# One decoder layer on one core: transfers at other places, two first tiles split from PSUM, squares of x later, last squares in two parts

## The chip, the cores and the metric

The kernel runs on one core of a Trainium2 chip. A core has a matrix engine (PE, with a queue of its own for weight loads, PEld), a vector engine (DVE), an activation engine (ACT), a general engine (POOL) and a queue engine (SP). SP's and POOL's DMA instructions move data between DRAM and the core's SBUF, over 16 DMA engines that all queues share. PE writes its results to PSUM, which DVE and ACT read. The metric is the device time of one execution in microseconds (us), as the median over several runs.

## The reference

One step of a hybrid decoder layer on 512 prompt tokens and 8 single tokens of running sequences, all in float32. Cut to what matters:

```
x = concat(x_prompt (1, 512, 2048), x_sample (8, 1, 2048))
proj = rmsnorm(x, norm_mix_g) @ w_in                 # 2048 -> 6160 columns
bg, cg, hin, q, k, v, og, glr = split(proj)
cu, conv_new = causal_dwconv(cg * hin, conv_prev, conv_w)     # width 3
ya = bg * cu                                         # 1024 columns
o, s_new = gla_chunked(q, k, v, log_sigmoid(glr @ gate_w2 + gate_b) / 16, gla_prev)
yb = rmsnorm(o per head) * gla_norm_g * silu(og)     # 4 heads, 1024 columns
x = x + concat(ya, yb) @ w_out
u, v = split(rmsnorm(x, norm_ffn_g) @ w_up)          # 2 x 5632 columns
cu, ffn_new = causal_dwconv(u, ffn_prev, ffn_conv_w)
x = x + (silu(cu + b) * v) @ w_down                  # 5632 -> 2048
y = rmsnorm(x, final_norm_g)
```

It also returns the new states. Those of the sample tokens (`new_conv_s`, `new_ffn_s`, two rows each) hold in row 0 what was row 1 of the old state: a copy from DRAM to DRAM.

## The kernel before

Tokens are columns: x and all that follows lies transposed, features on the 128 partitions, 520 tokens along, in two halves of 260. Each float32 operand is split in two parts of lower precision, hi and lo, and a product takes three matmuls (hi by hi, lo by hi, hi by lo). ACT makes hi by a copy, DVE makes lo as the difference. So each weight tile of 128 x 1024 (512 KB) passes ACT and DVE once before PE uses it.

The order of the instructions on PE, DVE and ACT is the order of the program text, cut in steps by calls of `in_order()`. The queues of SP and POOL run down their own lists, each instruction as soon as its data and its buffer are there.

**Start.** x arrives on SP's queue: the first 512 features in four loads (`x0` to `x3`), the others in three loads of 1 MB (`xc`). For each tile k of 128 features `x_copy(k)` has PE transpose the four blocks and the sample rows into a PSUM tile `tp` (2 buffers) and copies it to SBUF as `t`: on ACT for k < 4 (L382), on DVE after that. `x_split(k)` stores the copy to DRAM on POOL's queue (`xT_d`, L388; the residual reads it later) and splits it, scaled by the norm's weight `gm`: hi on ACT (L126, `bh` and `ch` for the two halves), lo on DVE (L127, `bl` and `cl`). `parts` splits a weight tile (L111, L112). The loop over k then runs 12 matmuls for each tile (L140), copies a tile ahead, splits another, and takes squares of x for the norm; those of the first 512 features are taken on POOL at k = 0 to 3, in place in `x0` to `x3` (L472). `warm(n)` issues n matmuls whose results are not used.

**Heads and convolution tiles** follow, and then 81 groups of seven products each, by a scheme that needs seven products of blocks in place of eight: 9 groups for the rest of `w_in` (mix), 8 for `w_out` (wo), 44 for `w_up` (up), 20 for `w_down` (down: 5 chunks c of input features by 4 groups g of output columns, written (c, g)). A product is 24 matmuls of 260 columns. `begin(n + 1)` at the first product (j = 0) of group n allocates and loads the four raw weight tiles of the next group: `weights` issues the tile (1,1) (L1140), `second_half` the two tiles (2,1) and (2,2) (L754); the tile (1,2) follows at j = 2 (`load_rest`, L1182). `prepare(i + 2)` makes hi (L1199), lo (L1203) and sums of tiles (L1144) two products ahead. For the first mix group the second half is loaded early, in the step before (`early`), and the sums of inputs that it multiplies come from DRAM as `yl<-mt_d` (L1579).

Before the group stage the two state copies (176 KB and 32 KB, L1109) are issued on POOL's queue.

**Down.** A product's inputs come from DRAM as `form` (L648, SP's queue). Results are added into 16 accumulators `acc[g, q]` in SBUF. The residual is added into them by DMA, with accumulation in the DMA, four for each g (`add_residual`, L1439, POOL's queue, from `x1_d`), at places given by (c, g) and j:

```
if j == 5 and (c, g) in ((1, 0), (1, 1), (1, 2), (2, 2)):
    add_residual("down", {0: 2, 1: 3}.get(g, c - 1))
```

Behind the last residual POOL's queue has `load_last`, eight loads of the last four tiles (L1446). Those four tiles of 44 are not in the groups; they run at the end in the usual way.

**End.** `half` runs the last products for a part of the tokens, adds the accumulators, transposes each tile of 128 features back (L1806), and after every fourth tile squares 512 columns on ACT with a sum (L1814). After m = 15 the sums are reduced (L1848), and the rows are scaled and stored.

## Time and profile before

| | |
|---|---|
| time before, median of 3 runs | 2170.77 us (2170.47 to 2171.22) |
| the profiled execution | 2170.91 us, of which its span is 2169.2 us |
| PE busy | 2137.6 us (99%) |
| DVE busy | 1735.3 us (80%) |
| ACT busy | 1112.6 us (51%) |
| POOL busy | 440.2 us (20%) |
| bytes moved by DMA | 415.51 MB, mean 192 GB/s |
| DMAs of the residual in the down stage (L1439) | 16 of 260.0 KB, 6.8 us to landing |

All times in the views count from the start of the span. [...] `[1.71 <-ACT ms L1233]` behind a row means that the engine was idle for 1.71 us before it and that the named instruction ended the idle time. A row with `x24` stands for 24 instructions in a run. In the tables of loads, the last number is the median time from issue to landing.

### The profile page before, as it was taken

What the parts mean: (1) busy time and instruction counts of PE and PEld (TensorE: products, weight loads), DVE (VectorE), ACT (ScalarE), POOL (GpSimd) and SP (SyncE); (2) the same over time, 40 slices, a digit from 0 to 9 for tenths busy, and PEclk for the clock granted to TensorE, in tenths of its full rate; (3) what the DMA queues carried; (4) which work ended last, traced back from release to release, by engine and by line L of the source; (5) the groups of instructions that cost most, each with busy time, mean ns of one, the idle gap of its engine ahead of it and who ended that gap; (6) DMA issues with size and microseconds to landing.
All of it is one profiled execution on the core that took longest, in us unless ns stands there. A gap on an engine that the chain in (4) does not pass through costs nothing.

```text
span 2169.2 us, 43815 instructions
## 1 busy us (share of the span) xinstructions
PE 2137.6 (99%) x17751; PEld 2114.4 (97%) x17751; DVE 1735.3 (80%) x2298; ACT 1112.6 (51%) x1625; POOL 440.2 (20%) x625
## 2 busy tenths in 40 slices
PE   9999999999999999999999999999999999999997
PEld 8999999999999998999999999999999999999997
DVE  6446465578888898998898998998998877888886
ACT  6335435345554577555555555555555553444445
POOL 4213131212243421121221131122111310010000
PEclk9999999999999999999999999999999999999999
DMA  8545464387898997667676676676677886894734
GB/s 248 144 129 156 125 187 121 99 241 204 208 258 248 297 269 188 175 179 190 166 189 177 166 196 177 166 199 174 174 185 189 292 204 192 249 272 135 227 108 157
DMA packets 467163, 415.51 MB, mean 192 GB/s; under 512 B 21641, under 2 KB 426393, under 8 KB 466817
## 3 DMA queue, kind: packets, MB, share of 16 engines
q1 hardware_dynamic: 424081, 289.71, 46.8%
q0 software_dynamic: 42832, 122.93, 21.6%
q8 instruction: 139, 2.28, 0.4%
q14 instruction: 63, 0.52, 0.1%
q10 hardware_dynamic: 48, 0.07, 0.0%
HBM read 299.45 MB, written 80.31 MB: 175 GB/s over the span
## 4 chain that ended last, share of the span: by engine, by line
PE 60%; DMA 2%; DVE 1%; issue 1%; ACT 0%; POOL 0%; ACTq 0%; DVEq 0%; POOLq 0%; SPq 0%
PE mm L1223 28%; PE ms L1223 11%; PE y L1466 7%; PE x L1466 6%; PE e L1466 2%; PE f L1466 2%; PE mm L140 2%; DMA x_d<-acc 1%; DMA ssq<-fh 1%; DMA raw<-in_w_down_dram 0%; PE ms L1806 0%; DVE lo L1203 0%; DVE yl L124 0%; ACT y L1864 0%; DVE s L1144 0%
## 5 line engine op out<-in xcount | busy, mean ns | idle before, releaser
L1223 PE MATMUL mm<-yl,hi 128*128 128x260 f32 x1696 | 477.2, 281 | 4.1 <-DVE yl L124 4.1
L1223 PE MATMUL mm<-yh,hi 128*128 128x260 f32 x1696 | 476.5, 281 | 1.9 <-ACT ms L1233 1.7
L1223 PE MATMUL mm<-yh,lo 128*128 128x260 f32 x1696 | 475.8, 281 | 1.3 <-DVE lo L1203 1.3
L1199 ACT ACTIVATE hi<-raw 128x1024 fp32r<-128x1024 f32 x324 | 342.0, 1056 | 243.7 <-issue 88.3
L1203 DVE TENSOR_TENSOR lo<-raw,hi 128x1024 fp32r<-128x1024 f32 x324 | 395.5, 1221 | 43.6 <-ACT hi L1199 40.6
L1203 DVE TENSOR_TENSOR lo<-s,hi 128x1024 fp32r<-128x1024 f32 x243 | 298.4, 1228 | 124.1 <-ACT hi L1199 123.8
L1199 ACT ACTIVATE hi<-s 128x1024 fp32r<-128x1024 f32 x243 | 257.5, 1059 | 222.6 <-PE ms L1223 93.9
L1223 PEld LDWEIGHTS mm<-yl,hi 128*128 128x128 f32 x1696 | 320.3, 189 | 4.9 <-DVE yl L124 4.9
L1223 PEld LDWEIGHTS mm<-yh,hi 128*128 128x128 f32 x1696 | 320.0, 189 | 2.3 <-ACT ms L1233 1.9
L1223 PEld LDWEIGHTS mm<-yh,lo 128*128 128x128 f32 x1696 | 319.7, 188 | 1.7 <-DVE lo L1203 1.7
L1223 PE MATMUL ms<-b,hi 128*128 128x260 f32 x1408 | 265.7, 280 | 0.0
L1223 PEld LDWEIGHTS ms<-b,hi 128*128 128x128 f32 x1408 | 222.6, 188 | 0.0
L1466 PE MATMUL y<-form,hi 128*128 128x260 f32 x1120 | 212.7, 282 | 1.3 <-DVE acc L1485 1.3
L1466 PE MATMUL x<-form,hi 128*128 128x260 f32 x1120 | 211.5, 281 | 0.1
L1144 DVE TENSOR_TENSOR s<-s,raw 128x1024 f32<-128x1024 f32 x162 | 197.9, 1222 | 2.8
L1223 PE MATMUL ms<-b,lo 128*128 128x260 f32 x704 | 197.9, 281 | 0.0
L1466 PEld LDWEIGHTS y<-form,hi 128*128 128x128 f32 x1120 | 177.6, 189 | 1.8 <-ACT hi L1199 0.8
L1466 PEld LDWEIGHTS x<-form,hi 128*128 128x128 f32 x1120 | 176.6, 188 | 0.7 <-issue 0.5
L1466 PE MATMUL y<-form,lo 128*128 128x260 f32 x560 | 157.4, 281 | 2.2 <-DVE lo L1203 2.2
L1466 PE MATMUL x<-form,lo 128*128 128x260 f32 x560 | 156.7, 280 | 0.3 <-DVE lo L1203 0.3
L112 DVE TENSOR_TENSOR lo<-raw,hi 128x1024 fp32r<-128x1024 f32 x76 | 93.1, 1231 | 75.3 <-ACT hi L111 75.3
L1223 PEld LDWEIGHTS ms<-b,lo 128*128 128x128 f32 x704 | 132.0, 188 | 0.0
(366 smaller groups left out, 5074.1 us busy)
## 6 DMA issues: line engine op xcount, KB each, us to landing
raw<-in_w_up_dram SPq DMA_DIRECT2D x176, 512.0 KB, 4.9
raw<-in_w_down_dram SPq DMA_DIRECT2D x96, 512.0 KB, 5.6
raw<-in_w_in_dram SPq DMA_DIRECT2D x92, 512.0 KB, 4.7
form<-f_d SPq DMA_DIRECT2D x126, 260.0 KB, 6.2
raw<-raw POOLq DMA_DIRECT2D x56, 512.0 KB, 5.8
f_d<-t POOLq DMA_DIRECT2D x80, 260.0 KB, 5.6
raw<-in_w_out_dram SPq DMA_DIRECT2D x32, 512.0 KB, 9.1
form<-g_d POOLq DMA_DIRECT2D x42, 260.0 KB, 7.4
```

Of the source, the lines that this page charges most:

```text
L112: nc.vector.tensor_tensor(lo, raw, hi.bitcast(F32), op=ALU.subtract)
L140: nc.tensor.matmul(o, w, xx, start=first and i == 0, stop=last and i == 2)
L1144: return lambda: nc.vector.tensor_tensor(out, x, y, op=ALU.add)
L1199: nc.scalar.activation(his[i], src, AF.Copy)
L1203: nc.vector.tensor_tensor(los[i], src, his[i].bitcast(F32), op=ALU.subtract)
L1223: nc.tensor.matmul(st["bank"][b], w[:, k, :], x, start=b not in st["used"] and k == 0 and j == 0, stop=k == 7 and j == 2, skip_group_check ...
L1466: nc.tensor.matmul(ps[:, m, :], w[:, k, m * P : (m + 1) * P], x, start=b not in st["used"] and k == 0 and j == 0, stop=k == 3 and j == 2, ...
```

## The change

Six edits, in the order of the program:

1. For k = 0 and 1 the hi part is computed on DVE from the PSUM tile (a multiplication by `gm`), and lo on DVE from the copy; ACT makes only the copy. The matmuls of k = 0 stand ahead of the loop as `first_pass(w, x)` (w and x: 0 is hi, 1 is lo), two passes before the transposes of tile 1 and one behind them. `warm(8)` is `warm(7)`.
2. The squares of the first 512 features on POOL are taken at k = 8 to 11.
3. The two state copies are issued in the up stage, at the product with index NW + 70 (NW is the index of the first up product).
4. The first mix group's raw tile (1,1) is loaded ahead of the second half and of two other loads.
5. The residual of the down stage is added at other places: for g = 1 at j = 1 of (1, 2), for g = 0, 2, 3 at j = 1 of (2, 1).
6. The squares of the last 512 columns at the end are taken in two parts, 384 columns after m = 14 and 128 after m = 15.

```diff
-            st = copies[k] = tmp()[:, :T]
+            st = tmp()[:, :T]
+            copies[k] = st, ps
...
-            if k < KD // 2:
+            if k < 2:
+                his, los = xa[k]
+                for hi, x in zip(his, halves(ps)):
+                    nc.vector.tensor_scalar(hi, x, gm[:, k : k + 1], None, op0=ALU.mult)
+                for hi, lo, x in zip(his, los, halves(st)):
+                    nc.vector.scalar_tensor_tensor(
+                        lo, x, gm[:, k : k + 1], hi.bitcast(F32),
+                        op0=ALU.mult, op1=ALU.subtract,
+                    )
+            elif k < KD // 2:
...
+        def first_pass(w, x):
+            for i, ps in enumerate(first):
+                for o, xx in zip(ps, xa[0][x]):
+                    nc.tensor.matmul(
+                        o[:, :HT], ws[0][w][:, 4 * i, :], xx, start=w == x == 0, stop=False
+                    )
...
-        warm(8)
+        warm(7)
         ws = [parts(raws[0], 8)]
+        first_pass(0, 0)
+        first_pass(0, 1)
         x_copy(1)
         x_split(1)
+        first_pass(1, 0)
...
-            for i, ps in enumerate(first):
+            for i, ps in enumerate(first if k else ()):
...
-            if c == 0:
+            if 8 <= k < 12:
                 nc.gpsimd.tensor_tensor(xc[0][t], xc[0][t], xc[0][t], op=ALU.mult)
-            elif c < 3:
+            if 0 < c < 3:
                 square(c, t)
...
-    for dst, src in ((new_conv_s, state_conv), (new_ffn_s, state_ffn_conv)):
-        nc.gpsimd.dma_start(dst[0, :, 0, :], src[0, :, 1, :])
...
     raws = [load_og(2), load_og(3)]
-    early = second_half(lambda m, k: mix_source(0, m, k))
+    w11, first = raw_tile(lambda m, k: mix_source(0, m, k), 1)
+    nc.sync.dma_start(*first)
+    early = {(1, 1): w11, **second_half(lambda m, k: mix_source(0, m, k))}
...
+        if i == NW + 70:
+            for dst, src in ((new_conv_s, state_conv), (new_ffn_s, state_ffn_conv)):
+                nc.gpsimd.dma_start(dst[0, :, 0, :], src[0, :, 1, :])
...
-            if j == 5 and (c, g) in ((1, 0), (1, 1), (1, 2), (2, 2)):
-                add_residual("down", {0: 2, 1: 3}.get(g, c - 1))
+            if j == 1:
+                for q in {(1, 2): (1,), (2, 1): (0, 2, 3)}.get((c, g), ()):
+                    add_residual("down", q)
...
-            if m % 4 == 3:
+            if m % 4 == 3 or m == KD - 2:
                 b = m // 4
+                c0, c1 = (0, 512) if b < 3 else ((0, 384), (384, 512))[m % 2]
                 for i, (u0, un) in enumerate(tiles):
                     junk = tmp()
+                    n = b + (c0 > 0)
                     nc.scalar.activation(
-                        junk[:un, :512], pt[0][i][:un, :], AF.Square,
-                        accum_out=sums[:un, i, b : b + 1],
+                        junk[:un, c0:c1], pt[0][i][:un, c0:c1], AF.Square,
+                        accum_out=sums[:un, i, n : n + 1],
                     )
```

`raw_tile` only allocates a tile of `weights` and names its source. Line numbers shift: L382 becomes L383, L1140's load of the first mix group L1648, L754 L774, L1182 L1206, L1579 L1603, L1439 L1463.

How the order on the engines changes, at three places. The first is ACT at the start, before:

```order
L382 ACTIVATE t<-tp 128x520
L126 ACTIVATE bh<-t,gm 128x260
L126 ACTIVATE ch<-t,gm 128x260
L111 ACTIVATE hi<-raw 128x1024
L382 ACTIVATE t<-tp 128x520
L126 ACTIVATE bh<-t,gm 128x260
L126 ACTIVATE ch<-t,gm 128x260
```

The same place of ACT in the change:

```order
L383 ACTIVATE t<-tp 128x520
L111 ACTIVATE hi<-raw 128x1024
L383 ACTIVATE t<-tp 128x520 x2
L126 ACTIVATE bh<-t,gm 128x260
L126 ACTIVATE ch<-t,gm 128x260
```

The hi part of the first weight tile moved ahead of the splits, two of which went to DVE. On PE the row of work at the start reads in the change:

```order
L360 MATMUL mm<-ones 128x128 x7
L460 MATMUL mm<-bh,hi 128x260
L460 MATMUL mm<-ch,hi 128x260
L460 MATMUL mm<-bh,hi 128x260
L460 MATMUL mm<-ch,hi 128x260
L460 MATMUL mm<-bl,hi 128x260
L460 MATMUL mm<-cl,hi 128x260
L460 MATMUL mm<-bl,hi 128x260
L460 MATMUL mm<-cl,hi 128x260
L378 MATMUL tp<-idn,x_142 128x128 x4
L379 MATMUL tp<-idn,xs 128x8
L460 MATMUL mm<-bh,lo 128x260
```

Before, the transposes of tile 1 (L378, L379) stood ahead of all products of tile 0; now eight of these stand before them and four behind them.

The second place is SP's queue at the start of the mix groups, before:

```order
L101 DMA raw<-in_w_in_dram 128x8x128 x6
L754 DMA raw<-in_w_in_dram 128x8x128 x2
L1626 DMA t<-o_d 128x520 x2
L1140 DMA raw<-in_w_in_dram 128x8x128
L1182 DMA raw<-in_w_in_dram 128x8x128
L1579 DMA yl_5224<-mt_d 128x520
```

And in the change:

```order
L101 DMA raw<-in_w_in_dram 128x8x128 x6
L1648 DMA raw<-in_w_in_dram 128x8x128
L774 DMA raw<-in_w_in_dram 128x8x128 x2
L1652 DMA t<-o_d 128x520 x2
L1206 DMA raw<-in_w_in_dram 128x8x128
L1603 DMA yl_5221<-mt_d 128x520
```

The load of tile (1,1) moved past four other loads.

The third place is POOL's queue in the down stage. Here the rows have the numbers of the tiles: before, 20909 to 20912 are the accumulators of g = 0, 21157 to 21160 of g = 1, 21390 to 21393 of g = 2, 21615 to 21618 of g = 3. Six rows of the sixteen, before:

```order
L1439 DMA acc_21393<-x1_d_117 128x2x260
L1439 DMA acc_21615<-x1_d_117 128x2x260
L1439 DMA acc_21616<-x1_d_117 128x2x260
L1439 DMA acc_21617<-x1_d_117 128x2x260
L1439 DMA acc_21618<-x1_d_117 128x2x260
L1439 DMA acc_20909<-x1_d_117 128x2x260
```

In the change the numbers are 20908 to 20911 for g = 0, 21156 to 21159 for g = 1, 21389 to 21392 for g = 2, 21614 to 21617 for g = 3:

```order
L1463 DMA acc_21159<-x1_d_117 128x2x260
L1463 DMA acc_20908<-x1_d_117 128x2x260
L1463 DMA acc_20909<-x1_d_117 128x2x260
L1463 DMA acc_20910<-x1_d_117 128x2x260
L1463 DMA acc_20911<-x1_d_117 128x2x260
L1463 DMA acc_21389<-x1_d_117 128x2x260
```

The sixteen DMAs stand behind each other on POOL's queue in both kernels; their sequence by g was 2, 3, 0, 1 and is now 1, 0, 2, 3.

## The prediction

> **What bounds the kernel now.** I read the page's busy times first, then a table of windows over the stretches that the change touches, and only then single rows of the timeline, the chain of waits and the DMA issues there.

> ```profile
> span 2169.2 us, 43815 instructions
> PE 2137.6 (99%) x17751; PEld 2114.4 (97%) x17751; DVE 1735.3 (80%) x2298; ACT 1112.6 (51%) x1625; POOL 440.2 (20%) x625
> ```

> PE, the matrix engine, is busy for 2137.6 of 2169.2 us. So 31.6 us of idle PE is all that a reordering can win back, beside time in which PE is busy at a lower clock or ahead of its first useful product. The windows (length, busy time and instructions of PE, weight load, DVE, ACT and POOL, then granted clock, DMA share, GB/s) say how much of that lies where the change works.

> ```profile
> 12.00:27.00 15.00, 13.74 (x92) 11.31 (x91) 12.55 (x15) 8.23 (x18) 7.52 (x10) 1.00 1.10 358
> 27.00:58.00 31.00, 30.43 (x245) 28.68 (x245) 23.53 (x41) 21.93 (x45) 16.15 (x45) 1.00 0.64 191
> 446.00:455.00 9.00, 9.00 (x78) 9.00 (x77) 2.60 (x4) 0.64 (x1) 0.78 (x2) 1.00 1.09 270
> 458.00:476.00 18.00, 14.41 (x101) 13.60 (x101) 16.69 (x21) 11.68 (x19) 0.00 (x0) 0.91 0.92 284
> 470.00:475.00 5.00, 5.00 (x32) 5.00 (x31) 5.00 (x6) 2.70 (x5) 0.00 (x0) 0.66 0.72 177
> 1798.00:1805.00 7.00, 4.78 (x27) 4.58 (x26) 6.25 (x7) 2.11 (x2) 1.81 (x2) 0.76 1.10 358
> ```

> At the start of the mix groups (458 to 476) PE is idle for 18.00 - 14.41 = 3.59 us, and after it the clock is 0.66 for 5 us. In the down stage one stretch of 7 us has 7.00 - 4.78 = 2.22 us of idle PE and a clock of 0.76. In both the DMA share is near or above 0.9. In 12 to 27, PE looks 92% busy, but its 15 us hold little work, as the rows below show.

> **The start: k = 0 and 1 split from PSUM, first products ahead of the loop, squares later.** The columns are start, duration, engine, line and operation, out and in, and the idle time before it with its releaser.

> ```profile
> 6.37 0.60 ACT L382 ACTIVATE t<-tp 128x520 f32<-128x520 f32 x1 [3.12 <-PE tp L379]
> 6.63 0.71 SPq L319 DMA_DIRECT2D xc<-in_x_prompt_dram  x1
> 7.83 1.04 ACT L111 ACTIVATE hi<-raw 128x1024 fp32r<-128x1024 f32 x1
> 8.93 0.39 PE L140 MATMUL mm<-bh,hi 128*128 128x260 f32 x1
> 12.16 0.38 PE L140 MATMUL mm<-bh,hi 128*128 128x260 f32 x1
> 16.47 0.60 PE L378 MATMUL tp<-idn,xc 128*128 128x128 f32 x4
> 18.73 0.60 PE L378 MATMUL tp<-idn,xc 128*128 128x128 f32 x4
> 19.53 0.66 PE L378 MATMUL tp<-idn,xc 128*128 128x128 f32 x4
> 20.05 1.66 DVE L127 SCALAR_TENSOR_TENSOR bl<-t,gm,bh 128x260 fp32r<-128x260 f32 x1 [0.58 <-ACT bh L126]
> 20.37 1.05 POOL L472 TENSOR_TENSOR x<-x 128x512 f32<-128x512 f32 x1
> 25.90 0.47 DVE L127 SCALAR_TENSOR_TENSOR bl<-t,gm,bh 128x260 fp32r<-128x260 f32 x1
> 27.05 0.39 PE L140 MATMUL mm<-bh,hi 128*128 128x260 f32 x1
> 29.26 0.39 PE L140 MATMUL mm<-bh,hi 128*128 128x260 f32 x1
> ```

> Before, ACT ran the copy of tile 0 (ends 6.97), two hi splits, and the hi part of the first weights at 7.83; PE's first product waited for that (8.93). With the two hi splits on DVE, ACT starts the weights at about 7.0, 0.8 earlier, and the first product stands near 8.1. From there PE has work without a gap: eight products of k = 0 (about 0.12 each, 24 to a 2.87 us row below, so 0.95), the transposes of tile 1 (0.80, as 18.73 to 19.53), four products with the low weights (0.47) and the transposes of tile 2 (0.80): k = 1 begins at 8.1 + 0.95 + 0.80 + 0.47 + 0.80 = 11.1 in place of 12.16, or -1.05. DVE pays for it with four short instructions for each of two tiles; they stand where DVE waited for ACT's hi, and the fall-back, if they delay the low weights, is a gain of 0, which I keep as the upper end.

> From k = 1 (12.16) to k = 6 (27.05) PE needs 14.89 us. The step from k = 6 to k = 7 takes 29.26 - 27.05 = 2.21, so five steps and one extra set of transposes come to 5 x 2.21 + 0.80 = 11.85. Some 3.0 us are lost there. The row at 20.05 says where: the same split that takes 0.47 at 25.90 takes 1.66 while POOL squares x (20.37, 1.05). Each of the four squares holds one split by about 1.2, and PE waits for that split. Moving the squares away frees up to 3.0.

> What takes it back: first, the load of the second quarter of x (1 MB, issued at 6.63) feeds the transposes at 16.47. These would now be wanted at about 14.8, and the window 12 to 27 has a DMA share of 1.10, so the load can't come sooner; I charge 0.5. Second, the squares now run at k = 8 to 11, in the window 27 to 58, where DVE is busy for 23.53 of 31 and PE loses 31.00 - 30.43 = 0.57 in all. If each square again holds a DVE instruction by 1.2, that is 4.8 us of DVE within 7.5 idle ones, spread over 9 us; I charge 0.2, and bound it by 0 and the old 3.0. Sum of the start: -1.05 - 3.0 + 0.5 + 0.2 = -3.3 (bounds -4.05 and 0).

> [...]

> **The start of the mix groups: first weights ahead, state copies away.**

> ```profile
> 436.10 1.22 DVE L112 TENSOR_TENSOR lo<-raw,hi 128x1024 fp32r<-128x1024 f32 x1
> 441.63 0.42 SPq L1140 DMA_DIRECT2D raw<-in_w_in_dram  x1
> 457.17 1.06 ACT L1199 ACTIVATE hi<-raw 128x1024 fp32r<-128x1024 f32 x1 [8.47 <-DMA raw<-in_w_in_dram]
> 459.60 1.92 ACT L123 ACTIVATE yh<-yl 128x520 fp32r<-128x520 f32 x3 [1.37 <-DMA yl<-mt_d]
> 468.50 0.39 PE L1223 MATMUL mm<-yh,hi 128*128 128x260 f32 x1 [1.71 <-ACT ms L1233]
> ```

> ```profile
> raw<-in_w_in_dram SPq DMA_DIRECT2D x92, 512.0 KB, 4.7
> ```

> The first mix weights are issued at 441.63 and release ACT at 457.17, 15.5 us later, where such a load lands in 4.7 as a rule. Behind them the sums (yl from mt_d) release ACT only at 459.60, and from there to 468.50 ACT and DVE work without pause: DVE is busy for 16.69 of 18 us. So the stall moves with the landing of the weights and of the first three sums. In the new order the weights are issued as soon as their buffer is free, after the low part at 436.10 to 437.3, ahead of two other loads, and the two state copies (176 and 32 KB, read and written) are gone from the queue beside. That takes 0.52 MB / 270 GB/s = 1.9 us and 0.21 MB or twice that / 270 = 0.8 to 1.6 us out of the crowded stretch ahead of the sums: they land 2.7 to 3.5 us sooner. I take 3.0 of the 3.59 us of waiting. The half clock that follows costs 5.0 x (1 - 0.66) = 1.7 us; DVE is full in these 5 us, so PE at full speed would mostly wait for DVE there, and I take 0.5 of it. Sum -3.5 (bounds 0, if the loads land no sooner, and -3.59 - 1.7 = -5.3).

> The copies themselves go to the up stage, where POOL has room.

> ```profile
> 1034.77 0.92 POOL L1148 DMA_DIRECT2D raw<-raw  x1 [13.43 <-DVE s L1144]
> ```

> POOL waits 13.43 us there; 208 KB behind each other delay nobody: 0. If that gap were gone, the next accumulating weight load would wait for two issues of about a us each.

> **Down: the residual.** The chain of waits (start, duration, what) has a group of seven products across the stall; the timeline rows follow.

> ```profile
> 1781.10 2.87 PE y L1466 x24
> ...
> 1787.71 10.29 DMA raw<-in_w_down_dram
> ...
> 1800.53 4.50 PE y L1466 x23
> 1805.04 2.90 PE x L1466 x24
> ```

> ```profile
> 1763.57 20.87 SPq L648 DMA_DIRECT2D form<-f_d  x20
> 1790.70 1.20 POOL L1439 DMA_DIRECT2D acc<-x_d  x1 [9.08 <-DVE acc L1485]
> 1800.53 0.39 PE L1466 MATMUL y<-form,lo 128*128 128x260 f32 x1 [2.22 <-DVE lo L1203]
> 1847.06 15.00 SPq L648 DMA_DIRECT2D form<-f_d  x20
> 1886.51 0.37 SPq L1182 DMA_DIRECT2D raw<-in_w_down_dram  x1
> 1905.44 1.05 ACT L1199 ACTIVATE hi<-raw 128x1024 fp32r<-128x1024 f32 x1
> ```

> A weight tile issued at 1787.71 takes 10.29 us to land, its low part is 2.22 us late for PE, and the next product runs at half speed: 23 matmuls in 4.50 us, where 2.87 x 23/24 = 2.75 are normal, so 1.75 more. The weights stand on SP's queue behind 20 form loads that took 20.87 us. The same 20 loads 83 us later, with no residual beside them, took 15.00. These 5.9 us are more than the 2.22 that were missing. In the change the residual DMAs of groups 2, 3 and 0 leave this stretch (a group's seven products take 7 x 2.87 = 20 us, and those named in the change begin at 1805 and 1865: so four DMAs come near 1810, the twelve others together from about 1870, when the form loads of 1847 have been issued). So the stall goes, with the slow product behind it: -2.22 - 1.75, taken as -3.9 (bounds -3.97 and 0, with -2.2 between if the clock falls all the same).

> What may be late next: the burst after 1870, twelve residuals and then eight loads of the last tiles, whose rows stand now at 1894 to 1912. A weight tile issued there at 1886.51 is read at 1905.44, 18.9 us later, so a landing of 10.29 is covered: 0.

> [...]

> **The tail.**

> ```profile
> 2157.40 0.60 ACT L1814 ACTIVATE t<-ms 128x512 f32<-128x512 f32 x1 [4.37 <-PE ms L1806]
> 2157.99 0.59 ACT L1814 ACTIVATE t<-ms 128x512 f32<-128x512 f32 x1
> ```

> These two squares stand between PE's last transposes and the end. Three quarters of each now go into two instructions that need only the tiles up to m = 14 and may run in the 4.37 us in which ACT waited. Two squares of a quarter remain; from 0.60 for 512 columns and no row for 128, I guess 0.3 each, which would be -0.6. But the long ones may still run when the last transposes are done, and then nothing is won. I take the middle, -0.3 (bounds -0.6 and 0).

> **Sum.** -3.3 - 3.5 + 0 - 3.9 - 0.3 = -11.0. The profiled execution took 2170.91 us, 1.7 around its span, and the median of the runs is 2170.77; 2170.8 - 11.0 = 2159.8, so 2160.0. About 0.2% (4.3 us, so 2166.4) is what a measurement here can tell from no change.

> **Rivals.**
> First, the squares are not what holds k = 1 to 5, or x arrives too late for the gain: the start brings 1.05 less 0.2, 2.4 less than summed, 2162.4. For it speaks the DMA share of 1.10; against it that each stretched split has a square beside it.
> Second, the clock falls in the down stage without the gap: 2159.9 + 1.75 = 2161.7. [...]
> Third, the mix start stays where it is, since DVE is busy there for 16.69 of 18 us and the DMA share near 1 (the same bytes, in another order): the 3.5 go, 2163.4.
> Fourth, the down stall comes back at the new burst with the same 3.9, and the mix start gives nothing: 2170.8 - 3.3 - 0.3 = 2167.2, which is no change by measurement.
> Fifth, slower: twelve residuals with eight loads hold up weights on the shared DMA engines from 1870 on. They would have to eat 18.9 us of lead and then 11 + 4.3 us of PE: it decides when a weight tile takes 34 us to land. The longest seen beside residuals is 10.29.

> **How the numbers follow.** All steps as summed 0.56; first rival 0.12; second 0.08; third 0.12; fourth 0.08; fifth 0.04. Faster takes the first four cases, 0.88; same 0.08; slower 0.04. The low end, 2157, is every bound at its best (4.05 + 5.3 + 3.97 + 0.6 = 13.9). The high end, 2166, holds the first and third rival together (2159.8 + 2.4 + 3.5 = 2165.7).

> **What would show it.** k = 1 near 11.1 and k = 6 near 23.7, with no split over 0.6 us ahead of k = 6 (else the start is wrong). The first mix weights' hi well ahead of 457, the products with yh from about 465 in place of 468.5 (else the mix step). Groups of seven down products all near 20 us, no gap over 1 us and a clock of 1.00 in 1780 to 1800 and in 1865 to 1915 (else the down step, or a new wait). A prediction that fails by more than its range would have its cause in a new gap of PE in one of these places.

## The result, and the profile after

The changed kernel takes 2161.14 us in the median of six runs (2159.76 to 2162.22), against 2170.68 us for the kernel before (six runs, 2169.87 to 2172.29): 9.5 us less. The ratio is 0.9955 with a 95% interval of 0.9942 to 0.9968. The forecast was 2160.0, with 2157 to 2166 as range. The profiled execution took 2160.99 us.

The page of the changed kernel, its first two lines:

```profile
span 2159.3 us, 43820 instructions
PE 2134.2 (99%) x17749; PEld 2112.2 (98%) x17749; DVE 1734.5 (80%) x2302; ACT 1111.6 (51%) x1631; POOL 439.7 (20%) x625
```

Idle PE has gone from 31.6 to 25.1 us, and busy PE from 2137.6 to 2134.2: part of the gain is time in which PE had worked at half clock (ahead of the tail, two stretches of 3.41 us before, from 470.4 and 1801.6, and one in the changed kernel, from 817.1). The windows of before, at the same places, and the stretch ahead of the last of them:

```profile
12.00:27.00 15.00, 14.99 (x113) 13.59 (x114) 11.47 (x21) 9.92 (x23) 3.56 (x7) 1.00 1.08 377
27.00:58.00 31.00, 29.81 (x241) 28.07 (x241) 24.08 (x39) 19.53 (x40) 21.11 (x54) 1.00 0.73 206
458.00:476.00 18.00, 15.83 (x127) 15.02 (x126) 17.88 (x25) 12.58 (x21) 0.57 (x1) 1.00 0.87 239
1777.00:1798.00 21.00, 21.00 (x179) 21.00 (x178) 17.98 (x18) 8.41 (x9) 0.00 (x0) 1.00 0.72 227
1798.00:1805.00 7.00, 7.00 (x61) 7.00 (x60) 5.65 (x7) 3.66 (x4) 0.00 (x0) 1.00 0.73 223
```

From 12 to 27 PE does 113 instructions in place of 92 and hardly waits (14.99 of 15); 27 to 58 has become worse by some waiting (29.81 of 31, where it was 30.43); the stall of the mix start is smaller in this trace and not gone. The work that stalled in the down stage before stands 5.75 us earlier now, and from 1777 to 1805 there is no gap and the granted clock is 1.00 (full; 0.50 is half).

Where the time came from is read from marks: the same instruction in both traces, and its shift. The rows are the first product of the heads (PE), and DVE's low part of the first product of four groups: the third mix group, the fourth up group, the fourth and the last down group. In each pair the kernel before stands first. The pairs:

```profile
58.01 0.38 PE L140 MATMUL mm<-bh,hi 128*128 128x260 f32 x1 [0.58 <-DVE k L524]
502.73 1.22 DVE L1203 TENSOR_TENSOR lo<-raw,hi 128x1024 fp32r<-128x1024 f32 x1
875.30 1.22 DVE L1203 TENSOR_TENSOR lo<-raw,hi 128x1024 fp32r<-128x1024 f32 x1
1754.37 1.22 DVE L1203 TENSOR_TENSOR lo<-raw,hi 128x1024 fp32r<-128x1024 f32 x1
2077.84 1.22 DVE L1203 TENSOR_TENSOR lo<-raw,hi 128x1024 fp32r<-128x1024 f32 x1
```

```profile
55.26 0.39 PE L140 MATMUL mm<-bh,hi 128*128 128x260 f32 x1 [0.58 <-DVE k L544]
497.49 1.22 DVE L1227 TENSOR_TENSOR lo<-raw,hi 128x1024 fp32r<-128x1024 f32 x1
869.56 1.21 DVE L1227 TENSOR_TENSOR lo<-raw,hi 128x1024 fp32r<-128x1024 f32 x1
1748.62 1.22 DVE L1227 TENSOR_TENSOR lo<-raw,hi 128x1024 fp32r<-128x1024 f32 x1
2068.08 1.22 DVE L1227 TENSOR_TENSOR lo<-raw,hi 128x1024 fp32r<-128x1024 f32 x1
```

| stretch | shift at its end | gained in it | forecast |
|---|---|---|---|
| start, to the heads | -2.75 | -2.75 | -3.3 |
| to the third mix group | -5.24 | -2.5 | -3.5 |
| to the fourth up group | -5.74 | -0.5 | 0 |
| to the fourth down group, past the state copies | -5.75 | 0.0 | 0 |
| to the last down group | -9.76 | -4.0 | -3.9 |
| to the end of the span | -9.9 | -0.2 | -0.3 |

These stretches are the measure of the experiments too: a total varies by 1.1 us (five executions with (1,1) back) to 6.1 us (23 of the kernel before) between executions of one kernel. From the fourth to the last down group the twelve kernels with the residual at its new places or left out agree to 0.01 (319.46 to 319.47); the landing of the first sums of the mix stage varies by 1.9.

### The profile page after: what moved, and what is told of

Read it like the earlier page. It is cut to its first block, busy times and chain, and to the rows that moved or that the text cites. A ratio compares the mean times of both kernels' runs of the same rounds, so it can differ in the third digit from the quotient of the medians.

```text
span 2159.3 us, 43820 instructions
## 1 busy us (share of the span) xinstructions
PE 2134.2 (99%) x17749; PEld 2112.2 (98%) x17749; DVE 1734.5 (80%) x2302; ACT 1111.6 (51%) x1631; POOL 439.7 (20%) x625
## 4 chain that ended last, share of the span: by engine, by line
PE 90%; DMA 3%; DVE 3%; ACT 1%; issue 1%; POOL 0%; SPq 0%; ACTq 0%; DVEq 0%; POOLq 0%
PE mm L1247 34%; PE mm L140 14%; PE ms L1247 14%; PE x L1490 9%; PE y L1490 9%; PE f L1490 3%; PE e L1490 3%; PE ms L982 1%; DMA form<-g_d 1%; DMA g_d<-t 1%; DMA yl<-t_d 0%; DMA yl<-mt_d 0%; PE ms L1836 0%; DMA raw<-raw 0%; PE ms L968 0%
## 5 line engine op out<-in xcount | busy, mean ns | idle before, releaser
L1223 ACT ACTIVATE hi<-raw 128x1024 fp32r<-128x1024 f32 x324 | 342.0, 1056 | 233.8 <-issue 89.4
L1223 ACT ACTIVATE hi<-s 128x1024 fp32r<-128x1024 f32 x243 | 257.4, 1059 | 220.7 <-PE ms L1247 93.6
L112 DVE TENSOR_TENSOR lo<-raw,hi 128x1024 fp32r<-128x1024 f32 x76 | 94.9, 1253 | 78.0 <-ACT hi L111 77.9
## 6 DMA issues: line engine op xcount, KB each, us to landing
raw<-in_w_up_dram SPq DMA_DIRECT2D x176, 512.0 KB, 4.6
raw<-in_w_down_dram SPq DMA_DIRECT2D x96, 512.0 KB, 4.7
raw<-in_w_in_dram SPq DMA_DIRECT2D x92, 512.0 KB, 4.5
raw<-raw POOLq DMA_DIRECT2D x56, 512.0 KB, 5.9
raw<-in_w_out_dram SPq DMA_DIRECT2D x32, 512.0 KB, 13.8
```

The costliest lines, as they stand in the source:

```text
L112: nc.vector.tensor_tensor(lo, raw, hi.bitcast(F32), op=ALU.subtract)
L1223: nc.scalar.activation(his[i], src, AF.Copy)
```

## The experiments

Each kernel is the changed one with the edit shown or named.

**Squares back at k = 0 to 3.** `if 8 <= k < 12` is `if k < 4`.

> The changed kernel with one part undone: POOL squares the first 512 features of x at k = 0 to 3 again, as before. Theory (each square that POOL runs beside DVE's splits stretches one split by about 1.2 us, and PE waits for the splits at k = 1 to 5): splits of 1.6 us come back ahead of k = 6, the 0.61 us wait at k = 12 of the changed kernel goes, and the first product of the heads stands about 2 us later than in the changed kernel (55.3, so near 57.3), the whole run about 2 us longer. Rival (the 3 us at k = 1 to 5 were the loads of x, and the squares do not matter): 55.3 to 55.6 and the same time.

Measured: 2164.37 us (ratio to before 0.9973, 0.9963 to 0.9982). A stretched split is back, beside its square; first DVE, then POOL:

```profile
19.45 1.66 DVE L127 SCALAR_TENSOR_TENSOR bl<-t,gm,bh 128x260 fp32r<-128x260 f32 x1 [0.58 <-ACT bh L126]
...
19.76 1.05 POOL L492 TENSOR_TENSOR x<-x 128x512 f32<-128x512 f32 x1
```

The heads begin at 57.37. By the transposes of tile 9, which lie behind the squares at k = 0 to 3 and ahead of those at 8 to 11, this kernel is at 27.96, and the changed kernel with six others that share its start are at 24.87 to 25.17, in the mean 25.03: 2.9 us. (A seventh was late for another reason, told in the last section.) Counted from the transposes of tile 2, ahead of every square, it is 17.71 us against 14.89 to 14.92, so 2.8: nearly the whole of the 3.0 that the prediction read from the stretched rows. The rival is out. The split began 0.31 us ahead of the square, and as in the kernel before (20.05 and 20.37) it was the one that was stretched, to 1.66 from 0.47, while the square kept its 1.05.

**Start back.** Splits of tiles 0 and 1 from ACT's copy, `first_pass` and the shorter `warm` undone.

> The changed kernel with the start alone undone: tiles 0 and 1 split by ACT and DVE from the copy, the 12 matmuls of k = 0 inside the loop, eight unused matmuls ahead. Theory (ACT's order sets the first product): k = 1 begins about 1 us later than in the changed kernel, counted from the copy of tile 0, and all that follows too: first product of the heads near 56.3 and the run about 1 us longer. Rival (the load of the second quarter of x holds k = 4 in any case, so an early start is only waited for there): the heads begin at 55.3 to 55.5 and the run is the same.

Measured: 2163.57 us, with the heads at 55.94, 0.7 later than in the changed kernel. (The total is 2.4 longer; what is left of that came behind the heads, where the two kernels are the same, and isn't explained by the edit.) k = 1 begins at 12.08, against 10.7 to 11.2 in the others with the early start, but for the late one, which is 0.9 to 1.4 us; but the transposes of tile 9, from this kernel and from the changed one, show half of it:

```profile
25.67 0.38 PE L378 MATMUL tp<-idn,xc 128*128 128x128 f32 x2
```

```profile
24.96 0.27 PE L378 MATMUL tp<-idn,xc 128*128 128x128 f32 x1
```

Against the mean of 25.03 the early start is worth 0.6 us at tile 9. The load of x is not what takes the rest, since the transposes of the second quarter run at 15.12 in the changed kernel without a wait. It is lost within k = 1, as the next run shows.

**hi of tiles 0 and 1 from the copy.**

```diff
-                for hi, x in zip(his, halves(ps)):
+                for hi, x in zip(his, halves(st)):
```

> The changed kernel with the hi parts of tiles 0 and 1 made by DVE from ACT's copy in SBUF and not from PSUM. Theory (DVE's first hi waits for ACT's copy anyway: in the changed kernel it begins at 6.48 and 10.23, just behind the copies that end at 6.44 and 10.20): nothing becomes later, k = 1 begins 10.7 to 10.9 and the heads at 55.1 to 55.4. Rival (reading PSUM is what makes the products early): the first product or k = 1 is later by the 0.6 us of a copy.

Measured: 2161.72 us, and tile 9 at 24.73, 0.3 ahead of the 25.03. DVE's hi of tile 1, in the changed kernel and here:

```profile
10.23 0.49 DVE L393 TENSOR_SCALAR bh<-tp,gm 128x260 fp32r<-128x260 f32 x1 [0.94 <-ACT t L383]
```

```profile
10.28 0.36 DVE L393 TENSOR_SCALAR bh<-t,gm 128x260 fp32r<-128x260 f32 x1 [1.02 <-ACT t L383]
```

Though it reads PSUM, DVE waits for ACT's copy of the same tile, and then takes 0.49 in place of 0.36 us. So nothing is won by the source. What makes the first product early is that ACT comes to the hi part of the weights sooner: it ends at 7.70 in the changed kernel and at 8.79 with the start back, and the first product follows it each time (7.75 and 8.85). In the changed kernel the products of k = 1 follow DVE's parts in small steps, 2.13 us from its first product to the next transposes (10.78 to 12.91) where the kernel with the start back takes 1.54: that 0.6 is the half of the early start that is lost. With the copy as source it is 1.89 (10.80 to 12.69), so 0.24 of the 0.6 is the source in PSUM; the rest stays with DVE's row of four parts.

**Squares on ACT, at k = 8 to 11.**

```diff
-                nc.gpsimd.tensor_tensor(xc[0][t], xc[0][t], xc[0][t], op=ALU.mult)
+                nc.scalar.activation(xc[0][t], xc[0][t], AF.Square)
```

> The changed kernel with the four squares at k = 8 to 11 taken by ACT (0.6 us each) in place of POOL. Theory (POOL's squares stretch DVE's instructions there by about 1.2 each, seen as 1.65 for the 0.42 of the low-rank difference and 2.44 for the 1.22 of a weight's low part, and PE waits 0.61 for it): all DVE instructions at their usual length, no wait at k = 12, the first product of the heads about 0.9 us earlier than in the changed kernel (near 54.4, x landing alike), the run 0.9 shorter. Rival (DVE is late there by its own load, not by the squares): the wait of 0.6 stays, and the heads begin at 55.2.

Measured: 2161.55 us, the heads at 54.58, 0.7 earlier. The total isn't shorter by the 0.9 that was expected; a gain of this size can't be seen in the totals. Groups of DVE by shape in the window 27 to 42, of the changed kernel and of this one (busy, mean ns):

```profile
L112 DVE TENSOR_TENSOR lo<-raw,hi 128x1024 fp32r<-128x1024 f32 x2 | 3.8, 1875 | 0.0
L298 DVE TENSOR_TENSOR wg<-wgraw,wg 128x256 fp32r<-128x256 f32 x1 | 1.6, 1646 | 0.0
```

```profile
L112 DVE TENSOR_TENSOR lo<-raw,hi 128x1024 fp32r<-128x1024 f32 x2 | 2.5, 1264 | 0.0
L298 DVE TENSOR_TENSOR wg<-wgraw,wg 128x256 fp32r<-128x256 f32 x1 | 0.4, 416 | 0.0
```

DVE's lengths are normal again and PE's wait at k = 12 is gone. From tile 9 to tile 15 this kernel takes 13.35 us and the changed one 14.23: at their new place the squares cost 0.88.

**Squares at k = 4 to 7.**

> The changed kernel with POOL's squares at k = 4 to 7. Theory (a square stretches whatever DVE instruction with two inputs runs beside it, and what that costs depends on how long ahead of PE the instruction is): at k = 4 to 7 DVE still feeds each tile directly ahead of its use, so the loss is that of k = 0 to 3 or near it, 2 us against the changed kernel (heads near 57). Rival (only k = 0 to 3 is tight, because the pipeline is just filling): 55.3 or earlier.

Measured: 2162.11 us, the heads at 56.21. One split is stretched to 1.82 us and PE waits 0.94 for it:

```profile
23.41 0.38 PE L140 MATMUL mm<-cl,hi 128*128 128x260 f32 x1 [0.94 <-DVE cl L127]
```

From the transposes of tile 2 to those of tile 15 it takes 29.69 us, against 28.24 with the squares on ACT, 29.12 in the changed kernel and 31.05 with the squares at k = 0 to 3. So the cost falls with the distance from the start: 2.8 at k = 0 to 3, 1.45 at 4 to 7, 0.9 at 8 to 11. The expected 2 us over the changed kernel were 0.95 at the heads, of which 0.4 already lies ahead of tile 2, where no square runs. Neither side had it.

**Tile (1,1) back behind the second half and o_d.**

> The changed kernel with the load of the first mix group's tile (1,1) back behind the two tiles of the second half and the two loads of o_d; the state copies stay in the up stage. Theory (0.52 MB ahead of the first sums cost 1.9 us of their landing, and the order of the weights costs what DVE must then do in a row): the first sums release ACT 0 to 1 us later than in the changed kernel, since the bytes ahead of them are the same in both orders, but the hi of tile (1,1) comes at 454 or later in place of 445.8 and the mix products stand 1 to 2 us later. Rival (the order does not matter, the copies did it all): tile (1,1) still lands before the sums, and the mix stage keeps its place, time as the changed kernel.

**State copies back ahead of the mix groups.**

> The changed kernel with the two state copies (208 KB from DRAM to DRAM) issued ahead of the mix groups again, while tile (1,1) stays first. Theory (0.21 MB moved once or twice beside the first sums): the first sums release ACT 0.8 to 1.6 us later than in the changed kernel, and the second mix group by the same. Rival (the order of the weights did it all, or the spread between executions covers both): the second mix group starts 442.2 to 443.7 us behind the heads' first product, as in the kernels where the copies were away.

**Both back.** (The edits of the last two together.)

> The changed kernel with both mix edits undone together: tile (1,1) behind the second half and o_d, and the state copies ahead of the mix groups. Theory (each alone is partly covered, since DVE's own chain follows, but together they delay tile (1,1) and the first sums by 2.5 us): the first sums release ACT near 401.6 us behind the heads' first product, as in the kernel before, against 398.7 to 400.6 in the kernels with both edits, and the second mix group begins near 444.7 us behind it, against 441.8 to 443.7. Rival (the mix gain is the spread of the loads and of the clock between executions): 442 to 443.7 here too.

Measured, counted from the heads' first product, with the kernel before and those that have both edits (eight executions: the changed kernel and the runs on other places; the expectations say second mix group where the mark is the third):

| kernel | first sums release ACT | third mix group | between them | clock at half behind the stall |
|---|---|---|---|---|
| before | 401.59 | 444.72 | 43.13 | yes |
| both back | 401.17 | 444.33 | 43.16 | no |
| (1,1) back | 400.35 | 443.50 | 43.15 | yes |
| copies back | 399.97 | 443.11 | 43.14 | yes |
| both edits | 398.65 to 400.56, mean 399.67 | 441.79 to 443.71, mean 442.8 | 43.14 to 43.17 | in 3 of 8 |

The times were 2162.56, 2163.34 and 2164.14 us for (1,1) back, copies back and both back. The third group stands 43.13 to 43.17 us behind the first sums in every row, whatever the order of the weights and whether the clock falls or not. With (1,1) back, ACT makes its hi at 453.09, nearly as late as expected, with both back at 454.03, and in the changed kernel at 445.84: the distance is the same. So the landing of the first sums is what counts here, and the half clock costs nothing that can be seen; the likely reason is that DVE is full there (busy for 3.42 of the 3.42 us at half clock in the kernel before, 470.38 to 473.80). PE's wait in front of the mix products is no measure of it: in five of the eight executions with both edits it is 1.71 us, as before. Both edits together move the landing by 1.5 us (401.17, one trace, to the mean of 399.67); the one trace lies 0.6 above the latest of the eight, and the totals with both back (2163.64 to 2166.65) lie above all of the changed kernel's. One alone can't be told from the spread of 1.9 us that the landing has between executions, so which of the two does how much stays open.

**Tile (1,2) behind the first three sums.** `load_rest(0)` follows the first three `load_sum`.

> The changed kernel with the load of the first mix group's tile (1,2) behind the first three sums in place of ahead of them. Theory (the first sums wait for the bytes ahead of them, 0.52 MB at 270 GB/s is 1.9 us, and all that DVE does after them follows): the first sums release ACT about 1.9 us sooner (near 452.4 in place of 454.3, heads alike), the waits of 1.2 to 1.7 and 0.4 us at the first mix products shrink or go, the second mix group 1 to 2 us earlier. Rival (the mix start is bound by DVE's own work of about 17 of 18 us): the sums come sooner and the products no sooner.

Measured: 2160.72 us. The first sums in the changed kernel and here:

```profile
454.32 0.64 ACT L123 ACTIVATE yh<-yl 128x520 fp32r<-128x520 f32 x1 [7.44 <-DMA yl<-mt_d]
```

```profile
453.36 0.64 ACT L123 ACTIVATE yh<-yl 128x520 fp32r<-128x520 f32 x1 [6.44 <-DMA yl<-mt_d]
```

From the heads that is 397.95, 1.7 before the mean of the kernels with both edits and 0.7 before the earliest of them, and the third group stands at 441.12, 1.7 before their mean and 43.17 behind the sums. So the mix start is still bound by when its sums land. The rival is right on DVE's chain behind them, which keeps its length, and wrong on what starts it.

**Residual of the down stage back.**

> The changed kernel with the residual of the down stage at its places of before. Theory (the residual DMAs beside the form loads of 1763 make the weights late): a wait of PE of about 2 us near 1788 and form loads of 20 or more us in place of 15, the run 2.2 us longer, and 4.0 if the clock falls after the gap. Rival (the stall of before was an accident of timing, by the shift of all that precedes): no wait over 1 us, and the time of the changed kernel.

Measured: 2165.60 us (0.9980, 0.9971 to 0.9989). From the fourth up group to the last down group it takes 1202.55 us, as the kernel before (2077.84 - 875.30 = 1202.54); the changed kernel takes 1198.52. The stall, and the form loads of this kernel and of the changed one:

```profile
1758.92 21.03 SPq L668 DMA_DIRECT2D form<-f_d  x20
...
1795.86 0.38 PE L1490 MATMUL y<-form,lo 128*128 128x260 f32 x1 [2.21 <-DVE lo L1227]
```

```profile
1757.41 15.91 SPq L668 DMA_DIRECT2D form<-f_d  x20
```

The place has moved by 4.7 us, and the stall is there to 0.01 us: no accident of timing. The theory holds.

**No residual in the down stage.** (The three lines that issue the sixteen DMAs are left out.)

> The changed kernel without the sixteen residual DMAs of the down stage (the residual is left out of the result). Theory (at their new places they cost nothing, since the weights of that stretch are ahead by more than a landing takes): the down stage from the twentieth up group to its end takes what it takes in the changed kernel, within 0.2 us, and no wait of PE changes there. Rival (the burst after 1870 still costs part of what the old places did, in waits too short to be listed): the stage is shorter by 0.5 us or more.

Measured: 2161.68 us, and 1198.53 us for the stretch, 0.01 from the changed kernel. At its new places the residual costs nothing, although a DMA of it there takes 9.3 us to land in the median, where it was 6.8.

**Three edits together:** squares on ACT, tile (1,2) behind the sums, hi from the copy.

> The changed kernel with three edits: the squares at k = 8 to 11 on ACT, the load of tile (1,2) behind the first three sums, hi of tiles 0 and 1 from the copy. Theory (each removes a wait of its own): the heads begin near 54.5, the second mix group 441.1 us behind that, the run 1.5 to 2.5 us shorter than the changed kernel, near 2159. Rival (the clock's fall at the start of the up stage and the opening of the gate at the start move the time by as much): 2160 to 2161.5.

Measured: 2158.53 us (five runs, 2157.42 to 2160.53), ratio to before 0.9944 (0.9932 to 0.9957). The heads begin at 54.19, the third mix group at 440.96 behind them. The first sum releases ACT at 397.29 from the heads, but ACT then waits another 0.65 us for the second one, and the third group stands 43.67 behind the first sum: here it is no longer the first sum alone that sets it. This is the fastest by its median, 2.6 us under the changed kernel; the two ratios' intervals overlap, so that it beats the changed kernel is likely and not shown by the totals alone.

## Why the prediction was right

- **Start, -3.3 forecast, -2.75 measured.** The mechanism held, the sizes of three terms did not, and they partly cancelled, which is luck. The early first product was put at -1.05; it came (k = 1 at 10.78, forecast 11.1), but is worth 0.6 at tile 9. The mistake is the step "DVE pays for it with four short instructions": it put DVE's row at nothing, and PE then followed that row part by part, 0.24 of the 0.6 that it lost by the source in PSUM. The 0.5 for the late second quarter of x was not needed. The 3.0 of the squares was nearly right (2.8; k = 6 at 23.43, forecast 23.7, and no split ahead of it over 0.49), but their new place costs 0.9, not 0.2: I set DVE's idle sum against the delay, while DVE had a weight's low part in its row there, which was stretched from 1.22 to 2.44, and what stands behind it is what PE needs next. In the changed kernel, DVE and then PE:

```profile
34.35 2.44 DVE L112 TENSOR_TENSOR lo<-raw,hi 128x1024 fp32r<-128x1024 f32 x1
...
38.12 0.39 PE L140 MATMUL mm<-xl,hi 128*128 128x260 f32 x1 [0.61 <-DVE xl L127]
```

- **Mix, -3.5 forecast, -2.5 in the two traces, -1.9 by the mean of eight.** "They land 2.7 to 3.5 us sooner" was too much: 401.59 against 399.67 is 1.9, and 1.5 of it by the run with both edits back. The step behind it is right, the groups follow the landing one for one; the 0.5 for the clock was wrong, it is worth 0 there. The trace of the changed kernel landed early among the eight (399.06), so its -2.5 flatters the term. The third rival, a mix start that stays where it is, is out: the landing moved, and the groups with it.
- **Clock.** The second rival, a fall of the clock in the down stage without the gap, did not come: 1777 to 1805 has 1.00, and there, where PE is the bound, the fall had cost its 1.8 us. The -0.5 from the third mix group to the fourth up group was not forecast and has no shown cause in the change: over the 14 traces this stretch takes 371.0 to 375.0 us, the longest two (374.2 and 375.0) with two windows of half clock at the start of the up stage.
- **Down, -3.9 forecast, -4.0 measured**, and both halves of the argument were tested: the residual back brings the stall back, the residual left out brings nothing more. The fourth and fifth rivals are out.
- **State copies, 0 and 0**, shown by equal shifts (-5.74 and -5.75) on both sides of them.
- **Tail, -0.3 forecast, -0.16 measured** (from the last down group to the end of the span 91.36 us before and 91.2 in every kernel with the change). A new wait takes part of it back: PE's last transposes write a PSUM tile that ACT is still squaring:

```profile
2147.57 0.33 PE L1836 MATMUL ms<-idn,t 128*128 128x128 f32 x1 [0.56 <-ACT t L1846]
```

## What to carry to other kernels

Compare the same instructions in two traces and read shifts stage by stage: in the down stage that resolves 0.1 us where totals scatter by 1 to 6, in the mix stage, where the loads themselves scatter (by 1.9), only about 2. In these traces a POOL square beside DVE's splits and differences is paid for by DVE: in the changed kernel the difference at 34.35 took 2.44 us in place of 1.22 and the one at 31.50 took 1.65 in place of 0.42, while the four squares kept 1.05 to 1.06 and DVE's copies from PSUM beside them (30.21 and 37.99) 0.70 and 0.69. So here it belonged where DVE is far ahead of PE (0.9 us lost at k = 8 to 11 against 2.8 at k = 0 to 3), or on ACT. A transfer that nobody waits for can still be the cause of a stall, by the queue of loads that it slows: the 20 form loads took 20.87 and 21.03 us with the residual beside them and 15.91 without, and PE's wait of 2.2 us came and went with that.

## What the runs showed of the hardware

```profile
466.97:470.38 3.41, 1.48 (x10) 1.28 (x11) 3.41 (x7) 2.85 (x6) 0.00 (x0) 1.00 1.21 296
470.38:473.80 3.42, 3.42 (x19) 3.42 (x18) 3.42 (x5) 1.95 (x4) 0.00 (x0) 0.50 0.57 122
818.50:821.91 3.41, 1.71 (x15) 1.50 (x14) 2.18 (x4) 2.33 (x6) 0.85 (x1) 1.00 1.10 328
821.91:825.33 3.42, 2.65 (x21) 2.45 (x22) 3.42 (x5) 2.81 (x5) 0.00 (x0) 1.00 1.16 267
```

```profile
813.73:817.14 3.41, 1.31 (x8) 0.91 (x8) 3.33 (x5) 3.41 (x7) 0.85 (x1) 1.00 1.14 332
817.14:820.56 3.42, 2.93 (x13) 2.94 (x14) 3.42 (x5) 2.68 (x5) 0.00 (x0) 0.50 1.14 266
```

Over the 14 traces, ahead of the tail (up to 2140), 18 windows at full clock had 1.80 us or more of idle PE, and the clock was at half in the next window each time; 37 had 0.8 to 1.70, and it never was; of three with 1.71 it fell in two. Half of 3.41 is 1.71. Two cases don't fit: twice the clock stayed at half for a second window, though PE had been idle for only 0.63 and 0.77 us of the first, and in the tail of one trace it fell behind 1.64. So in these traces it is not the length of one gap that counts, but the idle share of a window, and where the grid lies decides whether the same gaps bring 3.41 us of half clock. The gaps at the start of the up stage are nearly the same before and after (1.70 and 1.81 for the longest): before, the grid cut them so that no window was over half idle (1.70 us of 3.41 in the idlest; 2.10 in the changed kernel). The 1.75 us of the slow product in the prediction's down stage stood behind such a window (1.19 us busy of 3.41, 1798.17 to 1801.58): they went with the gap of 2.22 us, and with the residual back they came back with it (half clock from 1796.2 to 1799.6).

**The full clock is first on record at different times** (what the last expectation calls the opening of the gate). The trace's first record of the clock, at full, stands between 4.0 and 6.2 us in thirteen traces (6.17 before, 4.77 in the changed kernel) and at 10.3 in one, with the copies back, whose first product came at 9.30 in place of 7.7 to 8.0 in the others that start alike: its 14 unused matmuls ahead of that took 3.35 us (0.24 each), where the changed kernel's took 1.83 (0.13). Its heads began at 57.24, two microseconds late; this is part of the spread of the totals.
